# Input tiles ahead of the adaLN weights, one-column sums, and h from a kept transpose

## The chip, the cores and the metric

The kernel runs on one core of a Trainium2 chip (trn2). The metric is the device time of one execution in microseconds (us). The engines are TensorE (PE in the rows; PEld is its weight load), VectorE (DVE), ScalarE (ACT), GpSimd (POOL) and SyncE (SP), whose queue issues most DMA transfers. Each engine works through its own instructions in order and waits on semaphores for the others.

## What is computed

One layer of a hybrid encoder: 1024 positions, 1024 channels, one batch. The part that matters here is its head, before the two mixer branches:

```python
mod = (c @ w_ada + b_ada)[:, None, :]
shift, scale, gate = jnp.split(mod, 3, axis=-1)
h = (_layer_norm(x) * (1.0 + scale) + shift).astype(x.dtype)
p = h @ w_in + b_in                       # the combined input projection
...
h = jnp.sin(freq * (_hyena_pos_features(L) @ w1 + b1))   # the filter network
h = jnp.sin(freq * (h @ w2 + b2))
h = jnp.sin(freq * (h @ w3 + b3))
h = h @ w4                                # the implicit filters, times a decay
```

Behind it one branch is dilated windowed attention, the other a long convolution by FFT of size 2048 with those filters; both are gated, projected and merged.

## The kernel before

Everything is in one function, `hybrid_encoder`. `h` is kept transposed in two fp32r tiles of 128 x 8 x 1024, `hTh` (the value rounded) and `hTl` (the rest); index `kt` counts eight groups of 128 channels. Each projection (`proj`, L236) makes 48 products of 128x128 by 128x512 (L244): for each half of the positions eight groups times three, `wh` by `hTh`, `wh` by `hTl` and `wl` by `hTh`. Its weights come by `load_w` (512 KB) and are split by `split_w`, ScalarE writing `wh` (L224) and VectorE `wl` (L225).

The head runs in this order. SP first loads 16 tiles of `w_ada` (L314, 128x1024, 512 KB; two column halves `h`, eight row groups `kt`), through `WA` = 7 buffers that the first one-column products free again. `c @ w_ada` is a sum over all 1024 rows. VectorE forms the first three row groups of a half (`DVE_ROWS`, L406 and L408) in `accs`; TensorE takes the other five and `accs` as the moving side of 1-row products (`row_sum`, L319). `to_mods` copies the row to SBUF (ScalarE, L325), turns it into columns with eight products that have one moving column (L328), and VectorE adds the bias into `mods` (L329): eight shift columns, then eight scale columns.

Then SP loads the eight x tiles (L334) with the first weight tile of the projection between them. Each is normalized (VectorE's L428 and L430, three small GpSimd operations; the scaling on ScalarE in the first half, L437, on VectorE in the second, L434). For each of 16 pieces, TensorE transposes four 128x128 blocks into `px` (L442), ScalarE writes `hf` with scale and shift (L445) and `hTh` (L447), and VectorE `hTl` (L448). There are two `px` buffers.

The filter network `hidden` (L352) is a generator: three layers, two halves each. A piece is a 128x512 product on TensorE (L366, L368), six VectorE operations that reduce the argument (L371 to L376) and a sine on ScalarE (L377). Layers 1 and 2 are issued behind VectorE's last sum, layer 3 behind `h`; `hid`, its result, is read by the filters' products L573 and L574, and VectorE makes `g` of them (L576).

The order on each engine is fixed when the program is built. It is not the order of the code: a scheduler places each instruction when its operands are expected. `tc.issue_after(i)` lets what stands under it begin only behind instruction `i`. Pools with tags decide which tiles share memory.

Of the kernel before, what the change touches and what calls it, by code (L numbers as in the profile page):

```python
# [11 lines left out]
F32 = mybir.dt.float32  # L12
# [7 lines left out]
P = 128  # L20
# [19 lines left out]
XT = 8  # L40
WA = 7
DVE_ROWS = 3
# [124 lines left out]
def hybrid_encoder(ctx, tc, A):  # L167
# [25 lines left out]
    hTh = hpool.tile([P, KT, S], F32R, name="hTh")  # L193
    hTl = hpool.tile([P, KT, S], F32R, name="hTl")
# [78 lines left out]
    with ExitStack() as st:  # L273
# [18 lines left out]
        spx = sx.enter_context(tc.tile_pool(name="stx", bufs=2, reuse_waits="tile"))  # L292
        rows = sp.tile([P, 2, P], F32, name="rows")
# [15 lines left out]
        ps_r = [ps_z.tile([P, 512], F32, name="ps_r", tag="z") for _ in range(3)]  # L309
        ps_r.append(ps_w.tile([P, 512], F32, name="ps_r", tag="mm"))  # L310

        def load_wa(h, kt):
            wa = spx.tile([P, D], F32, name="wa", tag="wa", bufs=WA)
            last = SY.dma_start(wa, A["w_ada"][0][P * kt : P * kt + P, D * h : D * h + D])  # L314
            return wa, cols[:, CC + kt : CC + kt + 1], last

        def row_sum(h, v, w, start, stop):
            for q in range(2):
                PE.matmul(ps_r[2 * h + q][0:1, :], w, v[:, 512 * q : 512 * q + 512], start=start, stop=stop)  # L319

        def to_mods(h):

            srow = spx.tile([P, D], F32, name="wa", tag="wa", bufs=WA)[0:1, :]
            for q in range(2):
                ACT.copy(srow[:, 512 * q : 512 * q + 512], ps_r[2 * h + q][0:1, :])  # L325
            px = ps_x.tile([P, 512], F32, name="px", tag="px")
            for n in range(8):
                PE.matmul(px[:, n : n + 1], srow[:, P * n : P * n + P], ones[0:1, :], start=True, stop=True)  # L328
            V.tensor_tensor(mods[:, 8 * h : 8 * h + 8], px[:, 0:8], cols[:, BADA + 8 * h : BADA + 8 * h + 8], ALU.add)  # L329

        def load_x(b):

            xt = spx.tile([P, D], F32, name="xt", tag="xt", bufs=XT)
            return xt, SY.dma_start(xt, A["x"][0].rearrange("(p a) d -> a p d", a=8)[b])  # L334
# [60 lines left out]
        was = {}  # L395
        for h, kts in ((0, range(DVE_ROWS)), (1, range(DVE_ROWS)), (0, range(DVE_ROWS, KT)), (1, range(DVE_ROWS, KT))):
            for kt in kts:
                was[h, kt] = load_wa(h, kt)
                wa, cc, last = was[h, kt]
                if h == 0 and kt == DVE_ROWS:  # L400
                    net = hidden(feats)
                    with tc.issue_after(lastv.ins):
                        next(net)
                        next(net)
                if kt == 0:
                    V.tensor_scalar(accs[h], wa, cc, None, ALU.mult)  # L406
                elif kt < DVE_ROWS:
                    lastv = V.scalar_tensor_tensor(accs[h], wa, cc, accs[h], ALU.mult, ALU.add)  # L408
                else:
                    row_sum(h, wa, cc, kt == DVE_ROWS, kt == KT - 1)  # L410
                    if kt == DVE_ROWS + 1:
                        row_sum(h, accs[h], ones, False, False)
                        if h:
                            to_mods(0)
        to_mods(1)
        with tc.issue_after(last.ins):
            xts = [load_x(b) for b in (0, 4, 1, 5)]
        with tc.issue_after(xts[3][1].ins):
            ready[C_HY] = split_w(load_w(w_in[:, C_HY : C_HY + P]))
            xts += [load_x(b) for b in (2, 6, 3, 7)]  # L420
        with tc.issue_after(xts[7][1].ins):
            ready[C_HY + P] = split_w(load_w(w_in[:, C_HY + P : C_HY + 2 * P]))
        for half in range(2):
            for t in range(4 * half, 4 * half + 4):
                xt = xts[t][0]
                bst = spx.tile([P, 2, 6], F32, name="bst", tag="bst")
                for e in range(2):
                    V.bn_stats(bst[:, e, :], xt[:, 512 * e : 512 * e + 512])  # L428
                mv = spx.tile([P, 4], F32, name="mv", tag="mv")
                V.bn_aggr(mv[:, 0:2], bst)  # L430
                PO.tensor_tensor(mv[:, 2:3], mv[:, 1:2], epsc[:, 0:1], ALU.add)
                PO.tensor_tensor(mv[:, 3:4], mv[:, 2:3], epsc[:, 8:9], ALU.pow)
                if half:
                    V.tensor_scalar(xt, xt, mv[:, 0:1], mv[:, 3:4], ALU.subtract, ALU.mult)  # L434
                else:
                    PO.tensor_scalar(mv[:, 2:3], mv[:, 0:1], mv[:, 3:4], -1.0, ALU.mult, ALU.mult)
                    ACT.activation(xt, xt, AF.Identity, scale=mv[:, 3:4], bias=mv[:, 2:3])  # L437
            sl = slice(512 * half, 512 * half + 512)
            for kt in range(KT):
                px = ps_x.tile([P, 512], F32, name="px", tag="px")  # L440
                for a in range(4):
                    PE.transpose(px[:, a * P : (a + 1) * P], xts[4 * half + a][0][:, kt * P : (kt + 1) * P], ident)  # L442
# [6 lines left out]
        for _ in net:  # L449
            pass  # L450
# [806 lines left out]
```

## Time and profile before

| what | us |
|---|---|
| median of three runs | 1418.87 (1417.18 to 1422.88) |
| the profiled execution | 1418.57 |
| its span | 1416.8 |
| TensorE busy | 1346.5 (95%) |
| VectorE busy | 909.1 (64%) |
| ScalarE busy | 620.1 (44%) |
| GpSimd busy | 176.0 (12%) |

The span is the time from the first to the last instruction of the profile. A timeline row gives start, duration, engine, line, operation, the tiles written and read, a count (rows of one kind next to each other are joined) and, in brackets, the idle time ahead of it with what ended it. A product of fp32 operands leaves two records or more. Busy times of TensorE are pipelined, so that the durations of its records overlap; starts tell how dense they are.

### The profile page before, as it was taken

The page shows a single profiled execution, that of the slowest core. Times are in us where ns is not written, and L with a number is a line of the kernel's source. Part 1 is how long each engine was busy: PE and PEld are TensorE (multiplying, and loading weights), DVE is VectorE, ACT ScalarE, POOL GpSimd, SP SyncE. Part 2 cuts the span into 40 slices and gives each one's busy share as a digit, 9 for nine tenths or more (in the row PEclk, how much of TensorE's full clock was granted, in tenths as well). Part 3 has the DMA queues.
Part 4 walks back from the last instruction along what each step waited for, and adds up shares of the span by engine and source line. Part 5 has one row for each costly group of instructions (what it writes and reads, how often), then busy time and mean ns, then how long its engine had stood idle before and what let it go on. Part 6 is the DMA issues. An engine that isn't in the chain of part 4 may idle for free. (4 is left out here: it accounts for less than half of the span.)

```text
span 1416.8 us, 18336 instructions
## 1 busy us (share of the span) xinstructions
PE 1346.5 (95%) x6731; PEld 1088.7 (77%) x6731; DVE 909.1 (64%) x1705; ACT 620.1 (44%) x1217; POOL 176.0 (12%) x131
## 2 busy tenths in 40 slices
PE   5799998999899999999999999999999999898997
PEld 1477876777788787787988788878887898687886
DVE  5669785777989897845166714761476146328886
ACT  1565353534363534356265634663467335213200
POOL 0100002100000000231212112112211220123010
PEclk9899999999999999999999999999999999999999
DMA  7633544332112223131114421311131123557443
GB/s 248 210 105 117 171 160 152 108 135 82 56 52 93 75 87 101 36 94 31 37 54 120 109 61 60 94 32 46 60 75 39 49 75 98 162 165 225 114 114 68
DMA packets 148048, 140.62 MB, mean 99 GB/s; under 512 B 16211, under 2 KB 117999, under 8 KB 147702
## 3 DMA queue, kind: packets, MB, share of 16 engines
q1 hardware_dynamic: 146910, 134.84, 31.8%
q0 software_dynamic: 288, 4.19, 0.8%
q8 instruction: 53, 0.87, 0.3%
q10 hardware_dynamic: 760, 0.41, 0.1%
q14 instruction: 37, 0.30, 0.1%
HBM read 112.02 MB, written 27.40 MB: 98 GB/s over the span
## 5 line engine op out<-in xcount | busy, mean ns | idle before, releaser
L244 PE MATMUL pj<-hTh,wl 128*128 128x512 f32 x1024 | 407.9, 398 | 0.0
L244 PE MATMUL pj<-hTh,wh 128*128 128x512 f32 x1024 | 407.8, 398 | 0.0
L244 PE MATMUL pj<-hTl,wh 128*128 128x512 f32 x1024 | 407.1, 398 | 0.1
L225 POOL TENSOR_TENSOR wl<-wr,wh 128x1024 fp32r<-128x1024 f32 (+1 forms) x59 | 130.4, 2211 | 864.2 <-ACT wh L224 800.0
L244 PEld LDWEIGHTS pj<-hTl,wh 128*128 128x128 f32 x1024 | 193.7, 189 | 38.5 <-DVE hTl L448 0.6
L244 PEld LDWEIGHTS pj<-hTh,wh 128*128 128x128 f32 x1024 | 193.7, 189 | 37.1 <-issue 0.2
L244 PEld LDWEIGHTS pj<-hTh,wl 128*128 128x128 f32 x1024 | 193.5, 189 | 36.8
L224 ACT CAST wh<-wr 128x1024 fp32r<-128x1024 f32 (+1 forms) x88 | 85.5, 971 | 261.8 <-PE pj L244 113.6
L512 ACT CAST yh<-f 128x512 fp32r<-128x512 f32 x88 | 53.9, 614 | 79.3 <-DVE f L460 74.1
L1125 PE MATMUL pj<-y,wh 128*128 128x512 f32 x256 | 82.5, 404 | 0.0
L914 DVE TENSOR_TENSOR tmp<-pj,bv 128x512 f32<-128x512 f32 x16 | 11.1, 692 | 110.6 <-PE pj L903 110.6
L1195 PE MATMUL po<-wo,mh 128*128 128x512 f32 (+1 forms) x272 | 80.0, 378 | 0.0
L513 DVE TENSOR_TENSOR yl<-f,yh 128x512 fp32r<-128x512 f32 x88 | 61.7, 711 | 20.9 <-ACT yh L512 18.6
L933 ACT ACTIVATE sx<-sx,stat 128x256 f32<-128x256 f32 (+1 forms) x128 | 71.6, 563 | 3.3 <-DVE stat L931 3.0
L931 DVE CUSTOM_DVE_ANT_0 sx<-ss,tab 128x384 f32<-128x384 f32 (+1 forms) x112 | 53.8, 493 | 28.9 <-PE ss L859 17.9
L940 DVE TENSOR_TENSOR pt<-pp,pt 128x256 fp32r<-128x256 f32 (+1 forms) x128 | 61.9, 487 | 14.6 <-ACT pt L939 13.2
L903 PE MATMUL pj<-wh,hTh 128*128 128x256 f32 x256 | 70.8, 277 | 0.0
L903 PE MATMUL pj<-wh,hTl 128*128 128x256 f32 x256 | 70.7, 276 | 0.0
L903 PE MATMUL pj<-wl,hTh 128*128 128x256 f32 x256 | 70.7, 276 | 0.0
L939 ACT CAST pt<-pp 128x256 fp32r<-128x256 f32 (+1 forms) x128 | 52.4, 425 | 32.9 <-PE po L944 27.7
L534 PE MATMUL z<-yh,tcon 128*128 128x512 f32 x224 | 64.5, 404 | 0.0
L937 PE MATMUL pp<-ident,sx 128*128 128x128 f32 x320 | 58.3, 280 | 4.5 <-DVE pt L940 2.6
(224 smaller groups left out, 2382.5 us busy)
## 6 DMA issues: line engine op xcount, KB each, us to landing
wr<-in_w_in SPq DMA_DIRECT2D x64, 512.0 KB
wa<-in_w_ada SPq DMA_DIRECT2D x16, 512.0 KB
dk<-in_t_dec SPq DMA_DIRECT2D x32, 256.0 KB
h_dram<-hs SPq DMA_DIRECT2D x32, 256.0 KB
r_d<-thr SPq DMA_DIRECT2D x32, 256.0 KB
ht<-h_dram SPq DMA_DIRECT2D x32, 256.0 KB
thr<-r_d SPq DMA_DIRECT2D x32, 256.0 KB
xt<-in_x SPq DMA_DIRECT2D x8, 512.0 KB
```

Of the source, the lines that this page charges most:

```text
L224: ACT.copy(wh[:, :k, :], src)
L225: low[0].tensor_tensor(wl[:, :k, :], src, wh[:, :k, :].bitcast(F32), ALU.subtract)
L244: PE.matmul(ps, w[:, kt, :], h[:, kt, sl], start=i == 0, stop=i == len(ops) - 1)
L512: ACT.copy(yh[:, c, :], y)
L513: V.tensor_tensor(yl[:, c, :], y, yh[:, c, :].bitcast(F32), ALU.subtract)
L534: PE.matmul(z, m, v, start=k == 0, stop=k == 5)
L903: PE.matmul(ps[:, t % 2], h[:, 4 * q + k, P * t : P * t + P], w[:, 2 * k : 2 * k + 2, :], start=first and t % 2 == 0 and i == 0, stop=last ...
L933: ACT.activation(sx[:, : n * P], sx[:, : n * P], AF.Exp, bias=stat[:, t, e, 0:1], scale=-1.0, accum_out=stat[:, t, e, 1:2])
L937: PE.transpose(pp[:, a * P : (a + 1) * P], sx[:, a * P : (a + 1) * P], ident)
L940: V.tensor_tensor(pt[:, :n, 1, :], blk(pp), pt[:, :n, 0, :].bitcast(F32), ALU.subtract)
L1125: PE.matmul(ps, a[:, kt, :], b(kt), start=i == 0, stop=i == len(ops) - 1)
L1195: PE.matmul(po, m[kt][:, q], wos[kt][w][:, ds_], start=kt == 0 and i == 0, stop=kt == KT - 1 and i == 2)
```

## The change

- The eight x tiles are loaded first, into `xs`, which has the memory of `hTh`; then the 16 tiles of `w_ada`, eight of them into `was` (the memory of `hTl`), the others through the seven buffers; then two weight tiles of the projection.
- All eight x tiles are normalized on ScalarE in place (L411) and transposed at once (L416) into a kept `xT` (ScalarE, L417).
- VectorE sums six row groups of `w_ada` instead of three. Row groups 3 and 7 and the two `accs` go to TensorE as stationary side: `col_sums` (L327) makes one column of the result for each of eight 128x128 blocks. Three VectorE additions make `mods` (L433).
- `h` is made of `xT` without TensorE: ScalarE writes `hTh` (L441), the full value `hf` comes from VectorE (L445, 10 of 16) or ScalarE (L443, 6 of 16), VectorE writes `hTl` (L446).
- All three layers of the filter network are issued behind the last VectorE sum.

The core of the diff:

```diff
-    hTh = hpool.tile([P, KT, S], F32R, name="hTh")
-    hTl = hpool.tile([P, KT, S], F32R, name="hTl")
+    xs = hpool.tile([P, 8, D], F32, name="xs", tag="hTh")
+    was = hpool.tile([P, 8, D], F32, name="was", tag="hTl")
...
+        def col_sums(slot, h, v, w):
+            for n in range(8):
+                c = 16 * slot + 8 * h + n
+                PE.matmul(ps_m[:, c : c + 1], v[:, P * n : P * n + P], w, start=True, stop=True)
...
+        for t, b in enumerate(ORDER):
+            last = load_x(t, b)
+        with tc.issue_after(last.ins):
+            for kt in range(KT):
+                for h in range(2):
+                    wts[h, kt], last = load_wa(h, kt)
+        with tc.issue_after(last.ins):
+            ready[C_HY] = split_w(load_w(w_in[:, C_HY : C_HY + P]))
+            ready[C_HY + P] = split_w(load_w(w_in[:, C_HY + P : C_HY + 2 * P]))
+        xT = spt.tile([P, KT, S], F32, name="xT")
+        for t, b in enumerate(ORDER):
+            xt = xs[:, t, :]
...
+            ACT.activation(xt, xt, AF.Identity, scale=mv[:, 3:4], bias=mv[:, 2:3])
+            base = 256 * (b % 4)
+            for k in range(2):
+                px = ps_x.tile([P, 512], F32, name="px", tag="px")
+                for a in range(4):
+                    PE.transpose(px[:, a * P : (a + 1) * P], xt[:, (4 * k + a) * P : (4 * k + a + 1) * P], ident)
+                ACT.copy(xT[:, 4 * k : 4 * k + 4, base : base + 256].rearrange("p k (e j i) -> p k e j i", e=2, j=2)[:, :, :, b // 4, :],
+                         px.rearrange("p (k i e) -> p k e i", k=4, e=2))
+        acc_kts = [kt for kt in range(KT) if kt not in PE_ROWS]
+        for kt in range(KT):
+            cc = cols[:, CC + kt : CC + kt + 1]
+            for h in range(2):
+                if kt in PE_ROWS:
+                    col_sums(PE_ROWS.index(kt), h, wts[h, kt], cc)
+                elif kt == acc_kts[0]:
+                    V.tensor_scalar(accs[h], wts[h, kt], cc, None, ALU.mult)
                 else:
+                    lastv = V.scalar_tensor_tensor(accs[h], wts[h, kt], cc, accs[h], ALU.mult, ALU.add)
+                if kt == acc_kts[-1]:
+                    col_sums(len(PE_ROWS), h, accs[h], ones)
+        for slot in (0, 2, 1):
+            V.tensor_tensor(mods, ps_m[:, 16 * slot : 16 * slot + 16], cols[:, BADA : BADA + 16] if slot == 0 else mods, ALU.add)
...
-                px = ps_x.tile([P, 512], F32, name="px", tag="px")
-                for a in range(4):
-                    PE.transpose(px[:, a * P : (a + 1) * P], xts[4 * half + a][0][:, kt * P : (kt + 1) * P], ident)
...
+                ACT.activation(hTh[:, kt, sl], xT[:, kt, sl], AF.Identity, scale=sc, bias=sh)
+                if kt % 3 == 1:
+                    ACT.activation(hf, xT[:, kt, sl], AF.Identity, scale=sc, bias=sh)
+                else:
+                    V.tensor_scalar(hf, xT[:, kt, sl], sc, sh, ALU.mult, ALU.add)
                 V.tensor_tensor(hTl[:, kt, sl], hf, hTh[:, kt, sl].bitcast(F32), ALU.subtract)
-        for _ in net:
-            pass
+        with tc.issue_after(lastv.ins):
+            for _ in hidden(feats):
+                pass
```

Where it moves instructions, three places. On TensorE, the end of the adaLN sum in the order of before; `ps_r` is the row, `wa_258` and `wa_283` hold its copy, `xt` is a normalized x tile:

```order
L319 MATMUL ps_r_137<-acc_133,ones_78 1x512
L328 MATMUL px_261<-ones_78,wa_258 128x1 x8
L319 MATMUL ps_r_136<-wa_271,cols_74 1x512
...
L328 MATMUL px_286<-ones_78,wa_283 128x1 x4
L442 MATMUL px_360<-ident_72,xt_296 128x128
L328 MATMUL px_286<-ones_78,wa_283 128x1 x4
```

and the same place after; `px_362` and `px_368` take the last x tile, `px_506` and `px_517` are layer 1 of the filter network, `pj_594` is the first projection:

```order
L416 MATMUL px_362<-ident_72,xs_80 128x128 x4
L416 MATMUL px_368<-ident_72,xs_80 128x128 x4
L327 MATMUL ps_m_137<-cols_74,was_81 128x1 x8
L347 MATMUL px_503<-ident_72,frow_134 128x4
L359 MATMUL px_506<-feat_151,w1_128 128x512
L327 MATMUL ps_m_137<-ones_78,acc_135 128x1 x8
L327 MATMUL ps_m_137<-ones_78,acc_136 128x1 x8
L359 MATMUL px_517<-feat_152,w1_128 128x512
L327 MATMUL ps_m_137<-cols_74,wa_189 128x1 x8
L327 MATMUL ps_m_137<-cols_74,wa_191 128x1 x8
L244 MATMUL pj_594<-hTh_437,wh_195 128x512
```

The transposes moved ahead of the sum, and five of the six groups of one-column products stand in a row behind the last of them.

On VectorE, from the last sum to the first `hTl` after the change; `f_508` and `f_519` are the first layer of the filter network:

```order
L429 SCALAR_TENSOR_TENSOR acc_136<-wa_187,cols_74,acc_136 128x1024
L348 COPY fcol_133<-px_503 128x4
L364 TENSOR_SCALAR f_508<-px_506,fcol_133 128x512
...
L433 TENSOR_TENSOR mods_82<-ps_m_137,mods_82 128x16
L369 TENSOR_SCALAR f_508<-f_508 128x512
L433 TENSOR_TENSOR mods_82<-ps_m_137,mods_82 128x16
L364 TENSOR_SCALAR f_519<-px_517,fcol_133 128x512
L225 TENSOR_TENSOR wl_196<-wr_193,wh_195 128x1024
L445 TENSOR_SCALAR hf_439<-xT_205,mods_82 128x512
L225 TENSOR_TENSOR wl_202<-wr_199,wh_201 128x1024
L446 TENSOR_TENSOR hTl_438<-hf_439,hTh_437 128x512
```

Before, four chains of the filter network (`f`) stood between the sums and the first `mods`, with the statistics of x behind; now one and the start of a second are near `mods` and the others stand behind.

On SP, the first loads after; before, the sixteen `w_ada` stood ahead of the x tiles:

```order
L314 DMA xs_80<-in_x 128x1024
L296 DMA rows_120<-in_conv_w 36x128
L314 DMA xs_80<-in_x 128x1024 x7
L321 DMA was_81<-in_w_ada 128x1024 x8
L321 DMA wa_177<-in_w_ada 128x1024
...
L321 DMA wa_191<-in_w_ada 128x1024
L231 DMA wr_193<-in_w_in 128x8x128
```

The x tiles moved from behind the weights to their front. Ahead of the first L573, TensorE's order has 126 products L244 before and 149 after.

## Rows read from the trace of the kernel before

**Rows 1.** The page, part 2: busy tenths of TensorE in 40 slices.
```profile
PE   5799998999899999999999999999999999898997
```
**Rows 2.** Timeline of VectorE: start, duration, line, tiles, count, idle ahead.
```profile
15.28 2.70 DVE L408 SCALAR_TENSOR_TENSOR acc<-wa,cols,acc 128x1024 f32<-128x1024 f32 x2 [1.81 <-DMA wa<-in_w_ada]
...
18.16 0.81 DVE L371 TENSOR_SCALAR f<-px,fcol 128x512 f32<-128x512 f32 x1
...
31.93 0.43 DVE L376 TENSOR_SCALAR f<-f 128x512 f32<-128x512 f32 x1
...
48.45 0.17 DVE L329 TENSOR_TENSOR mods<-px,cols 128x8 f32<-128x8 f32 x1 [3.31 <-PE px L328]
...
80.90 1.28 DVE L448 TENSOR_TENSOR hTl<-hf,hTh 128x512 fp32r<-128x512 f32 x2
...
103.50 1.29 DVE L576 TENSOR_TENSOR g<-px,dk 128x512 f32<-128x512 f32 x2 [2.11 <-PE px L574]
```
**Rows 3.** Timeline of TensorE, 46 to 62 us.
```profile
46.12 1.05 PE L328 MATMUL px<-ones,wa 1*128 1x1 f32 x8
...
54.76 1.97 PE L442 MATMUL px<-ident,xt 128*128 128x128 f32 x8 [0.66 <-ACT hf L445]
56.38 0.78 PE L244 MATMUL pj<-hTh,wh 128*128 128x512 f32 x1
...
61.09 0.60 PE L442 MATMUL px<-ident,xt 128*128 128x128 f32 x4
```
**Rows 4.** Windows: length, busy (records) of PE, PEld, DVE, ACT, POOL; clock, DMA, GB/s.
```profile
46.00:48.50 2.50, 2.41 (x18) 2.07 (x17) 0.05 (x1) 1.72 (x2) 0.00 (x0) 1.00 1.05 379
48.50:50.20 1.70, 0.55 (x3) 0.31 (x3) 1.60 (x5) 0.16 (x1) 1.01 (x3) 1.00 1.18 279
50.20:56.30 6.10, 2.92 (x11) 2.13 (x12) 4.05 (x7) 5.54 (x8) 1.70 (x5) 0.50 0.68 181
48.60:103.50 54.90, 47.13 (x215) 36.66 (x216) 40.31 (x76) 37.59 (x57) 5.81 (x15) 0.88 0.35 106
120.00:140.00 20.00, 18.72 (x86) 14.53 (x85) 19.98 (x35) 12.94 (x25) 1.90 (x3) 1.00 0.20 74
140.00:160.00 20.00, 19.16 (x101) 15.55 (x100) 10.38 (x18) 9.95 (x19) 0.00 (x0) 1.00 0.55 174
```
**Rows 5.** Waits of SP, 0 to 110 us: total, times, longest.
```profile
SPq L314 <- PE ps_r L319: 11.3, 3, 5.0
```
**Rows 6.** Window with TensorE's busy time, clock, DMA share and GB/s.
```profile
36.00:40.00 4.00, 4.00 (x17) 1.00 1.02 408
```
**Rows 7.** Groups of ScalarE, 0 to 90 us: busy, mean ns, idle ahead.
```profile
L445 ACT ACTIVATE hf<-px,mods 128x512 f32<-128x512 f32 x16 | 11.8, 779 | 5.7 <-PE px L442 5.7
L447 ACT CAST hTh<-hf 128x512 fp32r<-128x512 f32 x16 | 9.2, 621 | 0.0
L437 ACT ACTIVATE xt<-xt,mv 128x1024 f32<-128x1024 f32 x4 | 5.0, 1239 | 11.4 <-POOL mv L436 11.4
...
L377 ACT ACT_TABLE_LOAD x1 | 1.3, 1283 | 13.9 <-DMA w<-in_filt_w 13.9
```
**Rows 8.** Groups of VectorE, 0 to 90 us, same columns.
```profile
L448 DVE TENSOR_TENSOR hTl<-hf,hTh 128x512 fp32r<-128x512 f32 x16 | 10.4, 685 | 5.2 <-ACT hTh L447 5.2
L428 DVE BATCH_NORM_STATS2 bst<-xt 128x6 f32<-128x512 f32 x16 | 10.1, 665 | 0.0
...
L434 DVE TENSOR_SCALAR xt<-xt,mv 128x1024 f32<-128x1024 f32 x4 | 3.2, 807 | 0.7 <-POOL mv L432 0.7
L372 DVE TENSOR_SCALAR f<-f 128x512 f32<-128x512 f32 x6 | 2.5, 422 | 0.1
```
**Rows 9.** Timeline of TensorE at 18 us.
```profile
18.10 2.07 PE L366 MATMUL px<-feat,w 66*128 66x512 f32 x2 [2.63 <-DVE fcol L355]
```
**Rows 10.** Waits of TensorE, 60 to 300 us: total, times, longest.
```profile
PE z L534 <- ACT yh L512: 8.2, 3, 5.7
```
**Rows 11.** The copies of line L590: duration min, median, max.
```profile
L590 POOL COPY h<-hs x4: 697/2444/7893, 128.7 to 258.7; 128x256 f32<-128x256 f32 x4
```

More of the change, by code (lines that the diff above doesn't have):

```diff
@@ L39 @@
 SX_BUFS = 3
-XT = 8
 WA = 7
-DVE_ROWS = 3
+PE_ROWS = (3, 7)
 FILLS = (3, 1, 4, 4)
@@ L292, in hybrid_encoder @@
         spx = sx.enter_context(tc.tile_pool(name="stx", bufs=2, reuse_waits="tile"))
+        spt = sx.enter_context(tc.tile_pool(name="stt", bufs=1, reuse_waits="tile"))
         rows = sp.tile([P, 2, P], F32, name="rows")
@@ L308, in hybrid_encoder, with load_x @@
         accs = [sp.tile([P, D], F32, name="acc", tag=f"acc{h}") for h in range(2)]
-        ps_r = [ps_z.tile([P, 512], F32, name="ps_r", tag="z") for _ in range(3)]
-        ps_r.append(ps_w.tile([P, 512], F32, name="ps_r", tag="mm"))
+        ps_m = ps_w.tile([P, 512], F32, name="ps_m", tag="mm")
+        def load_x(t, b):
+            return SY.dma_start(xs[:, t, :], A["x"][0].rearrange("(p a) d -> a p d", a=8)[b])
         def load_wa(h, kt):
[L313 to L325, printed above, removed]
-            px = ps_x.tile([P, 512], F32, name="px", tag="px")
-            for n in range(8):
[L328 to L334, printed above, removed]
+            if 2 * kt + h < 8:
+                wa = was[:, 2 * kt + h, :]
+            else:
+                wa = spx.tile([P, D], F32, name="wa", tag="wa", bufs=WA)
+            return wa, SY.dma_start(wa, A["w_ada"][0][P * kt : P * kt + P, D * h : D * h + D])
+        def col_sums(slot, h, v, w):
+            for n in range(8):
+                c = 16 * slot + 8 * h + n
+                PE.matmul(ps_m[:, c : c + 1], v[:, P * n : P * n + P], w, start=True, stop=True)
         def hidden_loads():
@@ L394, in hybrid_encoder @@
         feats = hidden_loads()
[L395 to L408, printed above, removed]
-                else:
[L410 to L422, printed above, removed]
-        for half in range(2):
[L424 to L437, printed above, removed]
@@ new lines, in hybrid_encoder @@
+        for t, b in enumerate(ORDER):
+            xt = xs[:, t, :]
+            bst = spx.tile([P, 2, 6], F32, name="bst", tag="bst")
+            for e in range(2):
+                V.bn_stats(bst[:, e, :], xt[:, 512 * e : 512 * e + 512])
+            mv = spx.tile([P, 4], F32, name="mv", tag="mv")
+            V.bn_aggr(mv[:, 0:2], bst)
+            PO.tensor_tensor(mv[:, 2:3], mv[:, 1:2], epsc[:, 0:1], ALU.add)
+            PO.tensor_tensor(mv[:, 3:4], mv[:, 2:3], epsc[:, 8:9], ALU.pow)
+            PO.tensor_scalar(mv[:, 2:3], mv[:, 0:1], mv[:, 3:4], -1.0, ALU.mult, ALU.mult)
+            ACT.activation(xt, xt, AF.Identity, scale=mv[:, 3:4], bias=mv[:, 2:3])
[6 more added lines that the diff above has]
+                         px.rearrange("p (k i e) -> p k e i", k=4, e=2))
@@ L438, in hybrid_encoder @@
+        for slot in (0, 2, 1):
+            V.tensor_tensor(mods, ps_m[:, 16 * slot : 16 * slot + 16], cols[:, BADA : BADA + 16] if slot == 0 else mods, ALU.add)
+        hTh = hpool.tile([P, KT, S], F32R, name="hTh", tag="hTh")
+        hTl = hpool.tile([P, KT, S], F32R, name="hTl", tag="hTl")
+        for half in range(2):
             sl = slice(512 * half, 512 * half + 512)
             for kt in range(KT):
-                px = ps_x.tile([P, 512], F32, name="px", tag="px")
-                for a in range(4):
-                    PE.transpose(px[:, a * P : (a + 1) * P], xts[4 * half + a][0][:, kt * P : (kt + 1) * P], ident)
@@ L444, in hybrid_encoder @@
-                hf = spx.tile([P, 512], F32, name="hf", tag="hf", bufs=3)
-                ACT.activation(hf.rearrange("p (r e l i) -> p r e l i", r=2, e=2, l=2),
-                               px.rearrange("p (r l i e) -> p r e l i", r=2, l=2, e=2), AF.Identity, scale=mods[:, 8 + kt : 9 + kt], bias=mods[:, kt : kt + 1])
-                ACT.copy(hTh[:, kt, sl], hf)
+                sc, sh = mods[:, 8 + kt : 9 + kt], mods[:, kt : kt + 1]
+                hf = spt.tile([P, 512], F32, name="hf", tag="hf", bufs=3)
@@ L730, in fill @@
                     gate_r(j, lambda: hx.tile([P, 512], F32, name="thr", tag="thr", bufs=2))
-        with tc.issue_after(xts[7][1].ins):
+        with tc.issue_after(last.ins):
             x0 = conv_x(0, 0)
```

3 lines of the change are left out of this document (added).

## Prediction

> **What bounds the kernel now.** I read the page first. Of TensorE's 40 slices (35.4 us each) nearly all read 8 or 9 tenths; the first two read 5 and 7 [rows 1]. Whatever this change gives must come from those two slices, or from what they hand on. So a microsecond counts by what it does to TensorE's backlog of projection products (L244) until about 290 us; behind that, both kernels have the same order on TensorE.
>
> Then VectorE's timeline, for the dates on which all hangs. `mods` is complete at 48.45 + 0.17 = 48.6 us; VectorE waited 3.3 us for it. Four chains of the filter network's layers 1 and 2 ran from 18.16 on, when VectorE had nothing else. The last `hTl` is written at 82.2 us (80.90 + 1.28), and the first filter product `g` starts at 103.50 [rows 2]. Between the two, TensorE's timeline shows the transposes and, from 56.38 on, the first products among them [rows 3].
>
> Last the windows by stage, with the granted clock: 1.00 (2.4 GHz) at 46 to 50.2 us, then 0.50 (1.2 GHz) until the projection products ran densely. Directly ahead of the fall TensorE was busy 2.41 of 2.50 us, but with the one-column products of L328. VectorE is nearly full later: 19.98 of 20 us at 120 to 140 [rows 4].
>
> **Loads.** Before, SP waited 11.3 us in three waits for the TensorE products that freed a weight buffer [rows 5]. Now the eight x tiles go first and eight of the sixteen weight tiles have memory of their own, so nothing waits for TensorE. Undisturbed, the transfers moved 408 GB/s [rows 6], so one 512 KB tile takes 524288 / 408 = 1.29 us. The fifth tile starts VectorE at 15.28 [rows 2]; the eighth is then in at about 19 to 20 us, the sixteen weight tiles at 20 + 16 × 1.29 = 40.6 and the two projection weight tiles at 43.2. The Trainium skill ("DMA: Bandwidth & Descriptors", the table of limits at its head) gives about 358 GB/s of HBM for a core, by which a tile would take 1.46 us and the weights would end 2.7 us later; the row at 408 GB/s with one core running decides.
>
> **x normalized and transposed early.** ScalarE's first computing instruction stands behind the same 15 loads and the table load as before: 13.9 + 1.28 = 15.2 us. It then has eight normalizations of 1.24 us and sixteen copies of a 128x512 PSUM tile, between 0.62 (cast from SBUF) and 0.78 us (from PSUM, permuted) [rows 7]; I take 0.72, near the second, since these too read PSUM. That is 9.9 + 11.5 = 21.4, so `xT` could be done at 36.6. VectorE's statistics (16 of 0.665 us = 10.6 [rows 8]) and its twelve sums (2.70 us for two [rows 2], so 16.2 at most) end near 40 us, behind the last tile that they need. TensorE's transposes are paced by ScalarE.
>
> **The adaLN sum.** Six groups of eight one-column products replace the one-row products. They are all in TensorE's queue, with two 512-column products of the filter network between them, ahead of `mods`. The nearest row is L328, the same 128-column weight load and one moving column: eight records (four products) take 1.05 us at 2.4 GHz, so a group of eight costs 2.0 us [rows 3]. At 1.2 GHz no row shows it. A bound from above is twice that, 4.0; one from below comes from the transposes, eight in 1.97 us at 1.2 GHz against four in 0.60 at 2.4, a ratio of 1.64, so 3.3 [rows 3]. I take 3.5. The 512-column product took 2.07 us at 18 us [rows 9]; I take that for the low clock and half for the high.
>
> From about 33 us (ScalarE has normalized the eighth tile at 15.2 + 8 × 1.24 + 10 × 0.72 = 32.3) TensorE has in front of it four groups of four transposes, the six groups, and the two wide products.
> Low clock: 4 × 0.98 + 6 × 3.5 + 2 × 2.07 = 29.0, end at 62.0, `mods` at 62.6 behind one small VectorE addition.
> High clock: 4 × 0.60 + 6 × 2.0 + 2 × 1.03 = 16.5, end at 49.5, `mods` at 50.
>
> Which clock? The row of 46.0 to 50.2 us says that one-column products do not hold it: TensorE was almost fully busy with them and the clock fell at once [rows 4]. The early transposes are paced by ScalarE and so leave pauses, as did those of 50.2 to 56.3 us (busy 2.92 of 6.10), through which the clock stayed at 0.50 [rows 4]. So I take 1.2 GHz up to the first projection product. The Trainium skill ("TensorE: Matmul & The Clock Gate", Part 1: The HAM clock gate) says instead that the clock follows how busy the engine has lately been and rises after sustained activity; by that, 29 us of products back to back would raise it. That is the first rival.
>
> **h.** No transposes and no PSUM reads are left here. ScalarE has 16 casts to `hTh` and 6 of the `hf` (0.62 us each, the row of a 128x512 cast from SBUF [rows 7]), 13.6 us, and one weight cast ahead; VectorE has 16 subtractions of 0.685, 10 `hf` of 0.42 (a one-operand 128x512 operation) and two weight subtractions (about 1.3 each, twice the elements of a 0.685) [rows 8], 17.8 us, with pieces of a filter chain between. I take 18.5 us from `mods` to the last `hTl`: 81.1 us at the low clock against 82.2 before, 68.5 at the high.
>
> At the low clock TensorE begins the products at 66.6 instead of 56.4, but then has them alone: no transposes between (some 40, 0.15 to 0.25 us each, 8 us [rows 3]). Both have one start at 1.2 GHz. It comes out level, within 1 us, when `h` is complete.
>
> **The filter network.** All six chains now stand behind the last sum. The four of 18 to 32 us took 14.2 us of VectorE, then free [rows 2]. Of the six, two find VectorE idle while it waits for `mods`; four (14 us) instead of two (7) lie in the stretch up to `g`. Against these 7 us VectorE loses there the statistics of five tiles (7.7 us) and the four normalizations of the second half (3.2), and gains ten `hf` (4.2): work is level, but it starts 14 us later. In before VectorE was busy 40.3 of the 54.9 us from 48.6 to 103.5 [rows 4]. From 62.6 the same work ends between 102.9, without a pause, and 117.5, with all of them. I take half the pauses for `g`, 111: TensorE's order no longer interleaves `h` with transposes, but the six sines and wide products still alternate with VectorE's chains. TensorE meanwhile has 23 more projection products ahead of the first filter product (149 for 126 in the order), 23 × 0.22 = 5.1 us (0.22 us a record, 18.72 us for 86 [rows 4]), and two more wide products, 2.1. So 7.2 of the 7.5 us of `g`'s delay are covered. Past 140 us VectorE has pauses again (10.38 busy in 20 us [rows 4]) in which the rest of its delay goes. I leave 1 to 2 us of lost time on TensorE, mostly one more start at 1.2 GHz, half of a stretch of some 3 us.
>
> **Sum.** The profiled execution took 1418.57 us (span 1416.8 and 1.8 around it), 0.3 below the median. 1418.6 + 1.5 = **1420 us**.
>
> **Rivals.**
> *The clock rises.* If TensorE gets 2.4 GHz in the early transposes or the sums, `mods` comes at 50 to 53, `h` is complete at 68.5 to 71.5, 11 to 14 us earlier, with no delay of VectorE. Some of it is lost where TensorE later waits for VectorE's chain (8.2 us in three waits for `yh`, one of 5.7 [rows 10]). 10 to 14 kept: 1405 to 1409, central 1407. For it: TensorE is hardly idle from 33 us on. Against it: [rows 4].
> *VectorE becomes the bound (slower).* Place: from `mods` to the first `g`. If the four chains and their sines do not fit into the pauses, `g` starts at about 117, and 6 us more than my cover are lost, with one fall of the clock behind an idle TensorE (1.7 us): 1420 + 7.7 = 1428. It decides when `g` starts later than 113. For it: VectorE's full windows, and a GpSimd copy that took 7.89 us instead of 0.70 while VectorE ran densely, beside the 5.7 us wait [rows 10, 11]. The Trainium skill ("SBUF — State Buffer", Who interferes with whom) describes such a lock between the two engines; the row agrees with it.
> *The copy goes undisturbed.* That same copy may now fall between other VectorE work, and the 5.7 us go, with the start at 1.2 GHz behind them (about 1.7): 1420 − 7 = 1413.
> *The early loads change nothing*, because TensorE's order puts the sums last whatever arrives: about 1418.
>
> **How the numbers follow.** Forecast 0.50 (1416 to 1425 by the bounds of a group, 3.3 to 4.0 us, which move `mods` by −1 to +3), clock rises 0.25, VectorE bound 0.17, copy undisturbed 0.05, no effect 0.03. 0.5% is 7.1 us, about what a measurement tells from no change: faster is below 1411.8, slower above 1426. Faster: 0.25, 0.02 of the undisturbed copy and 0.02 of the forecast's lower edge, 0.29; slower: 0.17 and 0.03 of its upper edge, 0.20; same 0.51. The range takes the clock's case in down to 1405 and the bound VectorE to 1428; its own range for the forecast alone is 1415 to 1426.
>
> **What would show it.** In the profile after: transposes from 17 us, x landed by 20 and the last weight tile by 41 us; the granted clock before 66 us 0.50 (forecast) or 1.00 (first rival); a group of eight one-column products in 3.5 or 2.0 us; `mods` at 62.6 or 50; the last `hTl` at 81 or 69; first `g` at 111, or past 113 for the second rival. The prediction is wrong in its centre if `mods` comes before 56 us or if `g` starts earlier than 105.

## The result and the profile after

The changed kernel takes 1428.76 us (median of 14 runs, 1421.94 to 1433.17) against 1418.06 us for the kernel before beside it (14 runs). The ratio is 1.0065, 95% interval 1.0045 to 1.0085; it is made from all the runs and so is not the quotient of the two medians. By it the changed kernel is slower by about 9 us (by the medians 10.7). That is the upper end of the range, 1428, and 9 us above the forecast of 1420. The profiled execution took 1430.0 us, its span is 1428.2.

The page after, part 2, TensorE's slices and its granted clock (compare [rows 1]):

```profile
PE   3899988899899999999999999999999999898997
...
PEclk9599999999999999999999999999999999999999
```

The first slice has lost two tenths and the second gained one; of the later ones the sixth and the eighth (178 to 214 and 250 to 286 us) went from 9 to 8. So not all of the loss is at the head. The head itself went much as worked out. Windows of the changed kernel (length, busy time and records of PE, PEld, DVE, ACT, POOL; clock, DMA share, GB/s) and TensorE's timeline:

```profile
32.00:36.00 4.00, 3.93 (x25) 3.93 (x26) 4.00 (x4) 1.68 (x4) 0.00 (x0) 0.67 1.03 410
36.00:44.00 8.00, 8.00 (x33) 6.93 (x32) 4.31 (x5) 1.58 (x3) 0.00 (x0) 0.50 1.08 337
44.00:52.00 8.00, 8.00 (x34) 6.97 (x33) 1.56 (x4) 0.64 (x1) 0.00 (x0) 0.50 0.27 82
52.00:58.30 6.30, 6.30 (x30) 6.23 (x30) 0.00 (x0) 0.00 (x0) 0.00 (x0) 0.50 0.00 0
```

```profile
16.62 1.97 PE L416 MATMUL px<-ident,xs 128*128 128x128 f32 x8 [8.09 <-ACT xs L411]
...
24.13 1.15 PE L416 MATMUL px<-ident,xs 128*128 128x128 f32 x8 [0.51 <-ACT xT L417]
...
37.56 3.41 PE L327 MATMUL ps_m<-cols,was 128*128 128x1 f32 x16
...
60.64 0.79 PE L244 MATMUL pj<-hTh,wh 128*128 128x512 f32 x1 [2.31 <-ACT hTh L441]
63.77 0.79 PE L244 MATMUL pj<-hTl,wh 128*128 128x512 f32 x1 [2.34 <-DVE hTl L446]
```

A group of eight one-column products (16 records) takes 3.41 us at 0.50. TensorE is busy without a pause from 36 to 58.3 us, and the clock stays at 1.2 GHz all the while. VectorE's dates (compare [rows 2]):

```profile
59.51 0.17 DVE L433 TENSOR_TENSOR mods<-ps_m,mods 128x16 f32<-128x16 f32 x1
...
77.45 0.68 DVE L446 TENSOR_TENSOR hTl<-hf,hTh 128x512 fp32r<-128x512 f32 x1
...
108.28 1.29 DVE L575 TENSOR_TENSOR g<-px,dk 128x512 f32<-128x512 f32 x2 [0.64 <-PE px L573]
```

`mods` is complete at 59.7 us, the last `hTl` at 78.1, 4 us earlier than before. The 149th product L244 starts at 107.2 us (111.2 before), the 250th at 149.6 (152.9): up to there the changed kernel leads. The 300th is 2.6 us behind, the 350th 8.0, the 800th 9.6; the spans end 11.4 apart. Between lie the waits of TensorE for `yh`. In the long convolution TensorE's products `z` read `yh`, which ScalarE makes of VectorE's `f`; of `z` ScalarE makes `hs`, a piece of a filter's spectrum on its way to memory. Compare [rows 10] and [rows 11]:

```profile
PE z L533 <- ACT yh L511: 14.4, 4, 4.1
PE z L543 <- DMA tcon<-in_t_con: 3.5, 1, 3.5
```

```profile
L589 POOL COPY h<-hs x4: 4012/4848/4871, 134.0 to 265.5; 128x256 f32<-128x256 f32 x4
```

All four GpSimd copies (one for each filter) now take 4.0 to 4.9 us; before, 0.70, 0.86, 4.03 and 7.89. What hangs on one of them stands in four timelines of the changed kernel, GpSimd, ScalarE (two rows) and TensorE:

```profile
134.04 4.83 POOL L589 COPY h<-hs 128x256 f32<-128x256 f32 x1 [56.32 <-ACT hs L585]
...
141.99 1.24 ACT L585 ACTIVATE hs<-z 128x512 f32<-128x512 f32 x2 [4.73 <-DMA h_dram<-hs]
...
144.07 0.62 ACT L511 CAST yh<-f 128x512 fp32r<-128x512 f32 x1
...
144.74 1.20 PE L533 MATMUL z<-yh,tabf 128*128 128x512 f32 x4 [3.48 <-ACT yh L511]
```

The copy reads `hs`, which has two buffers. The write-out of the first buffer waits for the copy and a clearing behind it, ScalarE's third `hs` waits 4.73 us for that write-out, and ScalarE's `yh` stands behind it in its queue; TensorE waits 3.48 us. At the same place of the kernel before, with a copy of 0.86 us, ScalarE waits 0.72:

```profile
128.69 0.86 POOL L590 COPY h<-hs 128x256 f32<-128x256 f32 x1 [49.49 <-ACT hs L586]
...
133.00 1.25 ACT L586 ACTIVATE hs<-z 128x512 f32<-128x512 f32 x2 [0.72 <-DMA h_dram<-hs]
```

Of the four copies the first two were short before; the third and the fourth were long in both kernels. So the loss is made at the first two: the changed kernel leads by 3.3 us at the 250th product and is 8.0 behind at the 350th, which starts at 203 us.

From 100 to 300 us TensorE is busy 184.15 us before and 178.55 after, and its mean clock is 0.97 and 0.95. The granted clock falls to 0.50 in or just behind each such wait: at 146.0, 190.4, 234.8 and 275.7 us in the changed kernel, at 224.3 and 268.6 us before:

```profile
100.00:300.00 200.00, 184.15 (x859) 147.11 (x858) 151.30 (x242) 90.44 (x173) 18.11 (x13) 0.97 0.44 141
```

```profile
100.00:300.00 200.00, 178.55 (x819) 142.72 (x819) 147.77 (x230) 90.73 (x171) 23.23 (x13) 0.95 0.43 142
```

That is 5.6 us of idle time and about 0.02 × 180 = 3.6 us of clock, together 9.2. At 100 us the two kernels are level (6444 and 6443 records of TensorE still to come), so this is most of the 9.6 us by which the 800th product is late.

### The profile page after: what moved, and what is told of

Its sections match the earlier page's. It is cut to its first block, busy times and chain, and to the rows that moved or that the text cites. A ratio compares the mean times of both kernels' runs of the same rounds, so it can differ in the third digit from the quotient of the medians.

```text
span 1428.2 us, 18387 instructions
## 1 busy us (share of the span) xinstructions
PE 1345.9 (94%) x6747; PEld 1106.9 (77%) x6747; DVE 918.0 (64%) x1718; ACT 628.9 (44%) x1224; POOL 184.4 (13%) x135
## 5 line engine op out<-in xcount | busy, mean ns | idle before, releaser
L244 PE MATMUL pj<-hTh,wh 128*128 128x512 f32 x1024 | 408.4, 399 | 2.5 <-ACT hTh L441 2.3
L244 PE MATMUL pj<-hTl,wh 128*128 128x512 f32 x1024 | 407.8, 398 | 2.3 <-DVE hTl L446 2.3
L244 PE MATMUL pj<-hTh,wl 128*128 128x512 f32 x1024 | 409.6, 400 | 0.0
L244 PEld LDWEIGHTS pj<-hTl,wh 128*128 128x128 f32 x1024 | 194.0, 189 | 41.5 <-DVE hTl L446 2.8
L244 PEld LDWEIGHTS pj<-hTh,wh 128*128 128x128 f32 x1024 | 194.2, 190 | 41.0 <-ACT hTh L441 2.4
L244 PEld LDWEIGHTS pj<-hTh,wl 128*128 128x128 f32 x1024 | 193.9, 189 | 38.7 <-issue 1.0
L511 ACT CAST yh<-f 128x512 fp32r<-128x512 f32 x88 | 54.0, 614 | 84.3 <-DVE f L459 78.1
L512 DVE TENSOR_TENSOR yl<-f,yh 128x512 fp32r<-128x512 f32 x88 | 61.6, 708 | 29.0 <-ACT yh L511 23.5
L1124 PE MATMUL pj<-y,wl 128*128 128x512 f32 x128 | 52.2, 408 | 11.0 <-DVE mg L1133 6.0
```

What stands on the lines that cost most here:

```text
L244: PE.matmul(ps, w[:, kt, :], h[:, kt, sl], start=i == 0, stop=i == len(ops) - 1)
L511: ACT.copy(yh[:, c, :], y)
L512: V.tensor_tensor(yl[:, c, :], y, yh[:, c, :].bitcast(F32), ALU.subtract)
L1124: PE.matmul(ps, a[:, kt, :], b(kt), start=i == 0, stop=i == len(ops) - 1)
```

## Experiments

Theory **lock**: what is lost is lost where GpSimd's copy gets no turn beside VectorE. Rival **lag**: VectorE is late because four filter chains moved behind `mods`; the copy only shows it. Rival **sums**: `mods`, 11 us late by the low clock, costs the time. The kernel before ran beside all of them (medians 1418.1 to 1420.3); the interval is that of the ratio to it. Dates are of the profiled execution, and the last column counts all waits of TensorE for `yh`, of which [rows 10] gives the largest group before.

| run | median us | ratio to before | `mods` | first `g` | waits for `yh`, 60 to 300 us |
|---|---|---|---|---|---|
| before | 1418.06 | 1 | 48.6 | 103.5 | 9.0 in 4 |
| changed kernel | 1428.76 | 1.0065 [1.0045, 1.0085] | 59.7 | 108.3 | 14.4 in 4 |
| a_copy_act | 1406.65 | 0.9894 [0.9878, 0.9911] | 62.8 | 111.7 | none |
| b_copy_act | 1408.77 | 0.9920 [0.9904, 0.9935] | 48.3 | 103.1 | 0.6 |
| a_all_on_dve | 1418.66 | 0.9986 [0.9972, 1.0000] | 48.1 | 102.7 | 0.2 |
| a_hidden_early | 1438.12 | 1.0129 [1.0111, 1.0148] | 77.3 | 113.4 | 14.2 in 4 |
| a_act_rows0 | 1398.52 | 0.9855 [0.9826, 0.9884] | 48.1 | 102.9 | 0.2 |
| a_act_double | 1437.39 | 1.0132 [1.0102, 1.0163] | 81.2 | 128.3 | 2.0 in 2 |
| a_act_dummy | 1405.47 | 0.9909 [0.9881, 0.9938] | 59.5 | 108.1 | none |
| a_act_rows7 | 1398.88 | 0.9862 [0.9832, 0.9891] | 56.5 | 107.5 | none |
| b_act_hidlate | 1412.16 | 0.9951 [0.9933, 0.9969] | 46.2 | 110.4 | 0.4 |
| a_act_wfirst | 1410.30 | 0.9939 [0.9913, 0.9964] | 42.5 | 113.6 | none |
| a_act_rows0_hid | 1409.83 | 0.9937 [0.9914, 0.9959] | 68.6 | 104.6 | 0.9 in 2 |
| a_copy_dma | 1440.53 | 1.0154 [1.0130, 1.0177] | 61.3 | 109.9 | 16.3 in 5 |

### The copies on ScalarE, in both kernels

```diff
-                    PO.tensor_copy(h0, hs[:, 0, :])
-                    PO.tensor_copy(h0[0:1, :], hs[0:1, 1, :])
-                    PO.memset(hs[0:1, 1, :], 0.0)
+                    ACT.copy(h0, hs[:, 0, :])
+                    ACT.copy(h0[0:1, :], hs[0:1, 1, :])
+                    ACT.mul(hs[0:1, 1, :], hs[0:1, 1, :], 0.0)
```

> The changed kernel with the GpSimd copy of a filter's first spectrum rows (two copies and a memset behind ACT's hs) put on ScalarE. Theory lock: the four copies took 4.0 to 4.9 us each on GpSimd in the changed kernel (0.7 to 7.9 before) while VectorE ran without a pause; ScalarE waits for the write-out of that tile, TensorE for ScalarE's yh (14.4 us in four waits, and two more falls of the clock than before). It expects the four waits of 3.2 to 4.1 us to shrink below 1.5 each, 7 to 14 us gained: 1415 to 1422. Rival lag: VectorE itself is late, because four hidden-layer chains moved behind mods; the copy is only where it shows. It expects under 4 us gained: 1425 to 1430.

> The kernel before with the same three operations on ScalarE. Theory lock: of 8.2 us of waits for yh the 5.7 us go with the start at 1.2 GHz behind it, 1408 to 1413; the distance between the changed kernel and before, both with the copy on ScalarE, falls from 10 to under 4 us. Rival lag: 1416 to 1419, and the distance stays at 8 to 11 us.

Measured 1406.65 and 1408.77. The copies take 0.4 us, and the four waits are gone. The longest of TensorE's waits from 60 to 300 us that are left in a_copy_act:

```profile
PE z L543 <- DMA tcon<-in_t_con: 4.4, 1, 4.4
PE px L572 <- DVE g L575: 4.0, 6, 1.1
PE pj L244 <- DVE hTl L446: 2.3, 1, 2.3
PE pj L244 <- ACT hTh L441: 2.3, 1, 2.3
```

With the copies out of the way the change is no longer slower: 0.9894 against 0.9920, 2 us in its favour, with intervals that overlap. Lag falls as the main cause: `g` is as late as in the changed kernel (3.4 us later even) and 22 us are gained. That is more than the lock was priced at, though, and the edit also changes the scheduler's order on TensorE, VectorE and ScalarE, in both kernels, from the first filter (at 128 to 138 us) up to 280 to 380 us. So the 22 and the 11 us are not simply the price of the lock. Where they are gained can be read from TensorE's records in equal windows. First the kernel before and b_copy_act, then the changed kernel and a_copy_act:

```profile
220.00:300.00 80.00, 68.26 (x291) 54.20 (x292) 52.85 (x87) 35.43 (x68) 6.74 (x7) 0.91 0.45 151
```

```profile
220.00:300.00 80.00, 76.36 (x344) 60.63 (x343) 63.32 (x107) 41.91 (x85) 0.55 (x1) 0.98 0.44 150
```

```profile
140.00:300.00 160.00, 138.55 (x620) 110.10 (x619) 112.24 (x171) 71.03 (x139) 17.69 (x10) 0.93 0.45 151
```

```profile
140.00:300.00 160.00, 151.26 (x704) 120.48 (x704) 129.24 (x210) 82.59 (x170) 0.55 (x1) 0.98 0.47 157
```

From 100 to 220 us, with two short copies, the kernel before and b_copy_act make 568 and 565 records. In the next 80 us, which hold the two long copies and the waits behind them, they make 291 and 344. Counted by the records still to come, the distance there becomes 12 us and stays at 10 to 12 to the end: it is the whole gain. By the same count the changed kernel falls behind a_copy_act by 4.8 to 6.4 us at each of its four long copies. A further 5.5 us come between 370 and 390 us, where it waits 4.4 us for VectorE's `f` and a_copy_act 0.8. So most of the gain lies at the long copies, in both kernels.

### Sums on VectorE; filter layers early

```diff
-PE_ROWS = (3, 7)
+PE_ROWS = ()
...
-        for slot in (0, 2, 1):
+        for slot in range(len(PE_ROWS) + 1):
```

> The changed kernel with no weight row groups on TensorE: VectorE sums all eight, TensorE makes only the two groups of one-column products of accs. Four groups of 3.4 us leave the queue ahead of mods, VectorE gets four sums of 1.29 us more. mods at 51 to 53 instead of 59.7. Theory sums at the low clock: the loss is the late mods; 6 to 9 us gained, 1420 to 1423. Theory lock: mods come earlier but the copies are stretched all the same; between 0 and 4 us gained, 1425 to 1429.

```diff
+        net = hidden(feats)
+        next(net)
+        next(net)
         acc_kts = [kt for kt in range(KT) if kt not in PE_ROWS]
...
         with tc.issue_after(lastv.ins):
-            for _ in hidden(feats):
+            for _ in net:
```

> The changed kernel with layers 1 and 2 of the filter network issued ahead of the sums, so that their four chains run while VectorE waits for mods (12.7 us idle there); layer 3 stays behind the last sum. mods stays at 59 to 62. Rival lag: 14 us of VectorE leave the stretch behind mods, the first g starts at about 103 instead of 108.3; 5 to 9 us gained, 1420 to 1424. Theory lock: the first filter is earlier but the copies still take about 4.8 us; 0 to 4 us gained, 1425 to 1429.

The first gained 10 us, more than either theory expected; two things came together, `mods` at 48.1 and copies that happened to be short. The second lost 9 us more, against both theories. Its products of layer 2 stand on TensorE ahead of the sums and wait there for ScalarE's sine, so `mods` comes at 77.3. Copies of the two runs, and TensorE in the second:

```profile
L589 POOL COPY h<-hs x4: 787/840/852, 130.0 to 248.9; 128x256 f32<-128x256 f32 x4
```

```profile
L592 POOL COPY h<-hs x4: 728/4490/7822, 138.9 to 275.8; 128x256 f32<-128x256 f32 x4
```

```profile
56.92 1.95 PE L327 MATMUL ps_m<-ones,acc 128*128 128x1 f32 x16 [0.37 <-DVE acc L432]
64.06 2.07 PE L361 MATMUL px<-f,w 128*128 128x512 f32 x2 [5.19 <-ACT f L370]
65.92 3.41 PE L327 MATMUL ps_m<-ones,acc 128*128 128x1 f32 x16
```

The four kernels with GpSimd's copy make 16 copies. Nine took 4.0 to 7.9 us, and behind each of these TensorE waited 2.3 to 5.7 us for `yh`; seven took 0.70 to 0.86 us, and behind none of them did it wait more than 0.2 us for `yh`. Among these 16 nothing lies between short and long.

### Doubling the sums, or halving them

With the copies on ScalarE the price of the sums can be seen by itself. Once all groups on VectorE (the two edits above together), once row group 7 alone on TensorE, and once each product made twice:

```diff
-PE_ROWS = (3, 7)
+PE_ROWS = (7,)
...
-        for slot in (0, 2, 1):
+        for slot in (0, 1):
```

```diff
                 c = 16 * slot + 8 * h + n
-                PE.matmul(ps_m[:, c : c + 1], v[:, P * n : P * n + P], w, start=True, stop=True)
+                for _ in range(2):
+                    PE.matmul(ps_m[:, c : c + 1], v[:, P * n : P * n + P], w, start=True, stop=True)
```

> The changed kernel with the copies on ScalarE and all eight weight row groups summed on VectorE: both single edits together. Theory that mods' date is worth time once the lock is gone: mods at about 51 instead of 62.8, first product and last hTl 11 us earlier; 5 to 10 us below the run with the copies alone (1406.7), 1397 to 1402. Theory that VectorE's chain limits the stretch up to about 350 us whatever the head does: within 3 us of 1406.7, the lead is given back at the wait for the last filter's f, as in the run with all sums on VectorE (6.4 us there).

> The changed kernel with the copies on ScalarE and only row group 7 on TensorE as stationary side; group 3 is summed on VectorE. Two groups of one-column products (6.8 us) leave the queue ahead of mods, VectorE gets two sums more, in time that it waits. mods at 56 to 57. If mods' date counts: 3 to 6 us below 1406.7. If not: within 3 us.

> The changed kernel with the copies on ScalarE and each one-column product made twice: 48 more of them, 20.5 us at the 0.427 us that one product takes in the trace after, all ahead of mods. mods at about 83. If the date of mods is on the path, the time rises by 10 to 20 us over 1406.7; if TensorE's backlog only waits for VectorE later, by under 5. With the doubled products TensorE is busy without a pause for about 45 us: the granted clock stays at 0.50 there if one-column products do not raise it; if they do, it rises to 1.00 and the added time is 10 us or less.

Measured 1398.52, 1398.88 and 1437.39 against 1406.65. So `mods`' date is on the path, but not all of it counts. Two groups fewer (`mods` 6.3 us earlier) give 8 us, more than expected; four fewer (another 8.4 us) give no more. On TensorE a_act_rows0 is some 3.5 us ahead of a_act_rows7 up to 750 us and loses that in a wait for VectorE's `v` at 756 us (2.3 us), which a_act_rows7 does not have.

One distance is larger than the copies can explain. a_act_rows0 is a_all_on_dve with the copies on ScalarE and takes 20 us less, although a_all_on_dve had no long copy. There a_all_on_dve loses its time elsewhere, from 340 to 370 us (TensorE busy 23.6 us against 29.2, behind 6.4 us of waiting for `f`) and from 580 to 600 (14.8 against 20.0, behind 5.0 us of waiting for VectorE's `xx`). So a distance of two medians is no price of a long copy by itself; the place has to be looked up, as above.

The doubled sums cost 31 us, more than the 20.5 us of added products and more than expected. About 22.6 us of it are there by 360 us, and 5.8 more come by 400 us, behind 4.4 us of waiting for `f` (0.8 in a_copy_act); the order behind changes with the sums, and which part is whose was not separated. The clock did not rise in 30 us without a pause, windows of the doubled run:

```profile
50.00:60.00 10.00, 10.00 (x46) 9.48 (x44) 2.36 (x4) 0.00 (x0) 0.00 (x0) 0.50 0.00 0
60.00:70.00 10.00, 10.00 (x42) 8.97 (x42) 0.81 (x1) 0.00 (x0) 0.00 (x0) 0.50 0.01 2
70.00:79.80 9.80, 9.80 (x47) 9.75 (x46) 0.00 (x0) 0.00 (x0) 0.00 (x0) 0.50 0.00 0
```

### A copy for which nobody waits

```diff
                     SY.dma_start(h0_dram[hc, o], h0)
+                    PO.tensor_copy(h0, h0)
```

> The changed kernel with the copies on ScalarE and, behind the write-out of that tile, one GpSimd copy of 128x256 onto itself per filter that nothing waits for soon. It does the disputed work at almost the same place with nobody behind it. Theory lock with a wait: these copies take 4 us or more where VectorE runs without a pause, but the time stays within 3 us of 1406.7. If a stretched GpSimd copy itself slows VectorE, the time rises by 5 us or more.

The time stayed at 1405.47, but of the four copies only one was long (3.2 us), so it bounds little:

```profile
L593 POOL COPY h<-h x4: 592/598/3183, 137.2 to 254.1; 128x256 f32<-128x256 f32 x4
```

### One part alone: filter layers late, weights first, layers early without the lock

```diff
-                    with tc.issue_after(lastv.ins):
-                        next(net)
-                        next(net)
...
-        for _ in net:
-            pass
+        with tc.issue_after(lastv.ins):
+            for _ in net:
+                pass
```

> The kernel before with the copies on ScalarE and one part of the change alone: all three layers of the filter network issued behind the last VectorE sum and, by the scheduler, behind h. Its comparison is the kernel before with the copies on ScalarE, 1408.8. Theory that the moved chains are free (the prediction's step: level work, TensorE covered by more projection products): within 4 us, 1405 to 1413. Rival: 14 us more of VectorE between mods and the first g start g about 8 to 14 us later than 103.1 and cost 5 us or more: 1414 to 1420.

```diff
-        for t, b in enumerate(ORDER):
-            last = load_x(t, b)
         wts = {}
-        with tc.issue_after(last.ins):
-            for kt in range(KT):
-                for h in range(2):
-                    wts[h, kt], last = load_wa(h, kt)
+        for kt in range(KT):
+            for h in range(2):
+                wts[h, kt], last = load_wa(h, kt)
+        with tc.issue_after(last.ins):
+            for t, b in enumerate(ORDER):
+                last = load_x(t, b)
```

> The changed kernel with the copies on ScalarE and the loads in the old order: the sixteen weight tiles first, the x tiles behind them. Its comparison is 1406.7. The sums no longer stand behind the transposes on TensorE: mods at 40 to 46 instead of 60 to 63, but xT is complete at about 58 instead of 40. Theory that the later of mods and xT decides: h starts a few us earlier or as before, 1400 to 1407. Rival, that x ahead is what gives the head its time: 1410 or more.

> The changed kernel with the copies on ScalarE, all weight row groups summed on VectorE, and layers 1 and 2 of the filter network issued ahead of the sums. Its comparison is the same without the last edit, 1398.5. The run with the filter layers early alone put their products into TensorE's queue ahead of the one-column sums, which then waited for VectorE and ScalarE (mods at 77). Theory that this order is what costs: mods at 55 or later instead of 48, 5 us or more above 1398.5. Rival, that taking the chains out of the stretch up to g pays: 1390 to 1396.

The third run has the edits of a_act_rows0 and of a_hidden_early together. The filter layers behind `h`, alone, cost 3.4 us (1412.16 against 1408.77, with intervals that just touch): the first `g` comes 7.3 us later, 9 us later measured from `mods`, and TensorE covers more than half of it. With the weights first, `mods` comes at 42.5 but the first product only at 67.6, behind the transposes, and the time is 3.6 us above 1406.65: `x` ahead of the weights does give something, about that much. Layers early cost 11.3 us again (1409.83 against 1398.52). TensorE and the sums in that run:

```profile
48.92 4.21 PE L361 MATMUL px<-f,w 128*128 128x512 f32 x4 [5.25 <-ACT f L370]
60.64 4.17 PE L361 MATMUL px<-f,w 128*128 128x512 f32 x4 [7.51 <-ACT f L370]
64.64 3.72 PE L327 MATMUL ps_m<-ones,acc 128*128 128x1 f32 x32
```

The last row is the price at the high clock, which the prediction had only from L328: 32 records in 3.72 us, 1.86 for a group, at a mean granted clock of 0.95, here behind two wide products.

### No copy at all

```diff
-                    PO.tensor_copy(h0, hs[:, 0, :])
-                    PO.tensor_copy(h0[0:1, :], hs[0:1, 1, :])
-                    PO.memset(hs[0:1, 1, :], 0.0)
-                    SY.dma_start(h0_dram[hc, o], h0)
+                    SY.dma_start(h0_dram[hc, o][1:P, :], hs[1:P, 0, :])
+                    SY.dma_start(h0_dram[hc, o][0:1, :], hs[0:1, 1, :])
+                    PO.memset(hs[0:1, 1, :], 0.0)
```

> The changed kernel without the two copies: the rows that they gathered are written out by two DMAs straight from ScalarE's tile, and GpSimd only clears one row of it behind them. Moving the copies to ScalarE also changed the scheduler's order behind the first filter, so that run had two differences. Here ScalarE gets no work, GpSimd reads nothing from SBUF there, and the order differs again. Theory lock: the waits of TensorE for yh stay below 1.5 us each and the time is 1404 to 1412. Rival, that the order made by ScalarE's copies gave the gain: 1418 or more, with waits for yh of 2 us and more, since the clearing of the row now stands behind two transfers.

Measured 1440.53: lock's forecast failed, and the waits for `yh` that the rival named are there. That the order made by ScalarE's copies gave the gain does not follow, though, since `hs` is held again. The clearing stands behind the transfers and starts at 142.88, 7.5 us after the tile was written. The write-out of the other buffer, issued at 136.7, has not landed either, and ScalarE waits for it as long as in the changed kernel:

```profile
143.35 0.60 ACT L585 ACTIVATE hs<-z 128x512 f32<-128x512 f32 x1 [4.68 <-DMA h_dram<-hs]
```

So this run put another hold of the same length in the copy's place: 16.3 us of waits for `yh` with no GpSimd read at all. What costs TensorE time here is how long `hs` is held, by whatever holds it. The 12 us by which it is slower than the changed kernel are not explained by these waits. The two are within 3 us of each other up to 610 us; the rest is lost from there to 630 us, behind two stalls (3.9 and 3.7 us, for VectorE's `xx`) of its own order.

## Where the prediction held, and where it failed

- **Loads, transposes, sums.** Right: 410 GB/s; transposes from 16.6 us (17 said); VectorE's sums end at 39.4 (40); a group 3.41 us (3.5 taken). `mods` at 59.7, not 62.6: ScalarE's copies of `px` took 0.58 us, below the bound of 0.62 that I took from a cast out of SBUF, and the early transposes ran partly at 2.4 GHz. In the three other runs with the same head (a_copy_act, a_act_dummy, a_copy_dma) `mods` came at 59.5 to 62.8.
- **The clock.** Right for the sums, which is what counted, and the rival of a rising clock fell; but the row that I read it from did not show it. [rows 4] has 1.7 us between the products of L328 and the fall at 50.2 us in which TensorE was busy for only 0.55, so the fall can be put down to that pause as well. The L328 products themselves ran at 1.00, and so did the sums of a_act_rows0_hid (0.95) behind two wide products: the forecast for the sums was right partly by luck. Wrong for the early transposes: eight take 1.97 us at 16.6 and 1.15 at 24.1, so the clock rose there and fell again (0.67 from 32 to 36 us). The granted clock reads 1.00 from 15 to 23 us all the same, so there the durations decide. The Trainium skill ("TensorE: Matmul & The Clock Gate", Part 1) has the clock rise after sustained activity, by which the sums would have run fast; the doubled run, with 30 us of them without a pause at 0.50, does not agree.
- **h and the level start.** Right: 18.5 us from `mods` to the last `hTl`, as taken. TensorE was even 4 us ahead at the 149th product.
- **The filter network.** Right in kind: `g` at 108.3 (111 said, where half of the pauses gives 110), and the moved chains alone cost 3.4 us where I left 1 to 2. The point from which the slower rival was to decide, `g` later than 113, was not reached, yet the time is the one that it gave. Its 1428 came out by luck, through the other piece of its evidence, the copy, at another place than it named.
- **The step that failed** is the sentence that leaves "1 to 2 us of lost time on TensorE" behind 140 us, and with it the rival of the undisturbed copy. I had read the copy of 7.89 us and the wait of 5.7, counted them as a sign of a late VectorE, and asked otherwise only whether they might go away. There were two long copies of four before; in the changed kernel there are four of four, and each costs 3 to 4 us and a fall of the clock, 9.2 us more than before in sum where 1 to 2 were left. [rows 11] had a minimum of 0.70 us and a maximum of 7.89, so there were short copies to be lost.

What stays open: why a copy is short in one place and long in another. In all 16, VectorE runs with hardly a pause when the copy starts. The seven short ones all ended inside VectorE's next `yl` (L512), which then took 0.76 to 0.90 us instead of 0.69. What tells the two kinds apart is the date of that operation: it starts 0.47 to 0.51 us after a short copy and 0.55 to 0.68 us after a long one. VectorE's row behind the short copy of 128.69 us before and behind the long one of 134.04 us after:

```profile
129.20 0.89 DVE L513 TENSOR_TENSOR yl<-f,yh 128x512 fp32r<-128x512 f32 x1
```

```profile
134.59 0.68 DVE L512 TENSOR_TENSOR yl<-f,yh 128x512 fp32r<-128x512 f32 x1
```

So less than 0.1 us of VectorE's timing goes with a difference of 3 us or more; what makes it so was not tested. Of the nine long ones five ended inside the next operation on `y` (L620), two at a gap of 0.03 us between VectorE's operations, and two only when VectorE ran out of work. What in the change puts all four on the wrong side was not found. That GpSimd was kept waiting by VectorE is read from these overlaps; no run took VectorE's work away from beside a copy.

## What to carry to other kernels

A wait that shows in one of four like places is a coin that has fallen four times: ask what any change of timing does to the other three, and take the hold away rather than the bad luck; a_copy_dma shows that taking only the engine away can leave another hold. Here three lines that move a small copy to the engine that wrote its source, together with leaving the column sums to VectorE, make 1398.5 us, 1.45% below the kernel before (1.16 to 1.74%), while the change alone was a loss. Price one-column products by the clock of the stretch where they stand (0.43 us each at 0.50, 0.23 at 0.95): 22 and 30 us of them here ran at 0.50 throughout.

## What the runs showed of the hardware

- GpSimd's copy of 128x256 out of `hs` takes 0.70 to 0.86 us or 4.0 to 7.9 us beside VectorE operations with two operands in SBUF, of which each starts some 0.08 us before the one ahead of it ends; one of a tile onto itself took 3.2. The Trainium skill ("SBUF — State Buffer", Who interferes with whom) says that such a VectorE instruction contends with a GpSimd one that reads SBUF, and has the lock for the whole of one instruction; here a long copy lasted over some seven to thirteen of them, and ended at a gap of 0.03 us, inside one kind of operation, or when they ran out.
- TensorE busy 29.8 of 29.8 us with one-column products and two wide ones kept 1.2 GHz (0.50, a_act_double). At that clock such a product costs 0.43 us; at a mean of 0.95, 0.23 (a_act_rows0_hid).
- A copy whose data VectorE never touches still costs when it is one link of a hold: two `hs` buffers, a write-out behind the copy, and a ScalarE that works in order turned 4.8 us of GpSimd into 3.5 us of TensorE.
